# Output projection on scaled fp16 parts, attention outputs scaled one part later, and fp16 dummies at the beginning

## The chip, the cores and the metric

One Trainium2 chip, one NeuronCore. The metric is the device time of one execution in microseconds, the median of several runs. The kernel before took 1050.61 us, median of 3 runs between 1050.59 and 1055.38.

## The reference

One decoder layer for 512 prompt tokens, 16 learned meta tokens before them and 32 sample tokens (8 sequences of 4), 2048 features, everything in fp32:

```python
hn   = rmsnorm(h, pre_norm_w)                        # over 2048 features
proj = einsum('btd,de->bte', hn, w_in)               # 2048 -> 8192, in 8 parts of 1024
q, fz, i, za, bg, cg, xt, zb = split(proj)
# A: 8 heads, key and value width 128: a gated linear recurrence
f = lb + (1 - lb) * sigmoid(fz);  k = (1 - lb) * sigmoid(-fz);  v = i
S_t = diag(f_t) S_{t-1} + k_t v_t^T;   o_t = S_t^T q_t
o = rmsnorm(o, hgrn_norm_w) * silu(za)               # per head
# B: a causal convolution of width 3 over the tokens
yb = bg * conv3(cg * xt) * silu(zb)
mix = einsum('bte,ed->btd', concat([o, yb]), w_out)  # 2048 -> 2048
y = h + rmsnorm(mix, post_norm_w)
```

Returned are y for prompt and sample (without the meta tokens), and the new states of the recurrence and of the convolution.

## The kernel before

**The beginning.** Weights and tokens are loaded; the tokens are normalized and transposed on TensorE (`turn_x`, three transposes for each group of 128 features) and split into two fp16 parts, high and low. Meanwhile TensorE runs dummy matmuls (`keep_busy`) into a scratch tile `warm`: four on the second weight block as soon as that has arrived, and six on the identity after the matmul that adds up the weights' sums of squares (`scale_of_weights`). They are fp32, 128 columns wide. The first feature pair is computed on the first half of the tokens (280 columns) while the transposes still come, and then on the second half.

**The input projection** goes through 32 pairs of features (`pair`), 256 features each. Four 512 KB blocks of weights (11, 12, 21, 22) per pair are loaded by SP two pairs ahead (`load_pair`). Their squares are summed on ScalarE (`squares`), a matmul with ones (`scale_of_weights`, name pss) adds them up over the partitions, and VectorE makes a power of two of it, the scale (sc). Each block, or sum of blocks, is then scaled and split into two fp16 tiles: the high part on ScalarE, the low part on VectorE (`split_w`, L288 and L289). A product is three fp16 matmuls for each of 8 groups of 128 features (high by high, high by low, low by high: L351, L352, L353, 272 columns of tokens). Three pairs in four use seven products instead of eight (names ma, mc, md are their accumulators, e1 to e3 and sums in `put` their copies, L370). The preparation of the next pair is cut into steps (`prep_steps`), one of them at the start of each product, some in its middle.

**The eight heads** (recurrence, norm, gate: `attend` and `gate`) run as a side program, of which `tick` executes one part every 11 feature groups, between the matmuls of the projection. In `attend` the outputs po get their per-head norm factor from GpSimd's chain of 12 small operations (zur, L861 to L864); then two parts follow (i = 0 and 1), in the first of which ScalarE scales the four blocks of outputs (sq, L879). Each part also updates the state of the samples (dss, an fp32r matmul of 512 columns, L882). The last head's and the convolutions' results go into mixf, fp32, 16 groups of 128 features by 544 tokens.

**The output projection** has 8 slices of 256 features (dp), each going through four chunks c of four feature groups. For each chunk there are two `feat` (weights stationary, 288 columns: samples and half the prompt; the result yT is transposed back later) and two `toks` (tokens stationary, 256 columns of weights). Both are three matmuls for each feature group (L1058 to L1060 in `feat`, L1066 to L1068 in `toks`), with operands of type fp32r: mh and ml are mixf's high and low part (`split`, A.copy and a subtraction), wh and wl the weights' (`prep_to`, L184 and L185, four groups of 128 input features at a time, two tiles ahead). ScalarE takes the results out (`take_feat`, and in `take` a sum of squares for the post norm), VectorE multiplies them by the post norm's weights; `turn_y` transposes yT back (yps), and the residual is added and stored at the end.

Order: the text of the program gives each engine's order, that is, what `step`, `tick` and `due` emit first comes first; but what the built program holds differs from it in places. In the kernel before, ScalarE's sums of squares of a pair's weights stand up to a whole pair ahead of the step that emits them, in between the copies of accumulators.

Of the kernel before, what the change touches and what calls it, by code (L numbers as in the profile page):

```python
# [64 lines left out]
def hymba_kernel(  # L65
# [76 lines left out]
    wts = {}  # L142
# [13 lines left out]
    def load_pair(p):  # L156
        if p < NP:
            for key in ("11", "21", "22", "12"):
                load_w(p, key)
        elif p < NP + 4:  # L160
            load_to(2 * (p - NP) + 2)

    nld = npr = 0

    def load_to(n):
        nonlocal nld
        while nld < min(n, KT):
            for kc in range(KT // KC):
                raw = wpool.tile([P, KC, P], F32, name=f"rawo_{nld}_{kc}", tag="raw", bufs=6)
                dp, c = divmod(nld * 2 + kc, 4)  # L170
                src = w_out[0][c * SEQ:(c + 1) * SEQ, dp * W:(dp + 1) * W]
                nc.sync.dma_start(wide(raw), src.rearrange("(k p) e -> p k e", p=P))
                raws.setdefault(nld, []).append(raw)
            nld += 1

    def prep_to(n):
        nonlocal npr
        load_to(n)
        while npr < min(n, KT):
            for kc in range(KT // KC):  # L180
                raw = raws[npr][kc]
                wh = wpool.tile([P, KC, P], F32R, name=f"wh_{npr}_{kc}", tag="w", bufs=8)
                wl = wpool.tile([P, KC, P], F32R, name=f"wl_{npr}_{kc}", tag="w", bufs=8)
                A.copy(wh, raw)  # L184
                V.tensor_tensor(wl, raw, wh.bitcast(F32), op=ALU.subtract)  # L185
                wts.setdefault(npr, []).append((wh, wl))
            raws.pop(npr)
            npr += 1
# [76 lines left out]
    def scale_of_weights(p, cols=(0, 4), tag="tr"):  # L265
# [4 lines left out]
        pool = {"tr": ps_tr, "lv": ps_lv}[tag]  # L270
# [4 lines left out]
        G.tensor_scalar(sc[:, 1:2].bitcast(I32), sc[:, 0:1].bitcast(I32), -1.0, sxk[:, 1:2], op0=ALU.mult, op1=ALU.add)  # L275
        G.tensor_scalar(sc[:, 2:3], sc[:, 1:2], -1.0, None, op0=ALU.mult)
        return sc

    scs = {}

    def seven(p):
        return p >= PLAIN and p % 4 in SEVEN

    def split_w(p, key):
# [5 lines left out]
                               w[:, 0].rearrange("p k e -> p (k e)"), op0=ALU.mult, op1=ALU.subtract)  # L290

# [8 lines left out]
    def prep_steps(p):  # L300
# [29 lines left out]
        for key in ("11", "12", "21", "22"):  # L330
            yield lambda key=key: split_w(p, key)
# [44 lines left out]
    def pair(p, off, sink):  # L376
# [3 lines left out]
        nxt = list(prep_steps(p + 1)) if p + 1 < NP else [lambda: None] * 5 + [lambda: prep_to(1), lambda: prep_to(2)]  # L380
        due = iter(nxt)
# [102 lines left out]
    keep_busy(4, raws[0, "12"][:, 0, :])  # L484
    sc0 = scale_of_weights(0, (0, 2))
    keep_busy(6)
# [179 lines left out]
    def attend(h, f, kb, q, vt, g):  # L666
# [207 lines left out]
        for i in range(2):  # L874
            yield
            if i == 0:
# [29 lines left out]
        for hf in range(2):  # L906
            V.scalar_tensor_tensor(groups(mixf[:, h, 0:NS])[:, :, hf], groups(mps2[:, 0:NS])[:, :, hf], hnw,
                                   g[:, hf * (TH - 8):hf * (TH - 8) + 16].rearrange("p (g r) -> p g r", r=8),
                                   op0=ALU.mult, op1=ALU.mult)

    def conv(c, p0):
# [58 lines left out]
        for hf in range(2):  # L970
            V.tensor_tensor(mixf[:, 8 + c, 0:NS].rearrange("p (g h r) -> p g h r", h=2, r=8)[:, :, hf],
                            two(y)[:, hf, 0:16].rearrange("p (g r) -> p g r", r=8),
                            two(gz)[:, hf, 0:16].rearrange("p (g r) -> p g r", r=8), op=ALU.mult)

    for i in range(H):
        head(i, 4 * i, f0 if i == 0 else None)
        conv(i, 4 * i + 2)
# [6 lines left out]
    mh = [opa.tile([P, NOUT], F32R, name=f"mh{e}") for e in range(EARLY)]  # L984
    ml = [opa.tile([P, NOUT], F32R, name=f"ml{e}") for e in range(EARLY)]

    def split(e):
        A.copy(mh[e], mixf[:, e, :])
        V.tensor_tensor(ml[e], mixf[:, e, :], mh[e].bitcast(F32), op=ALU.subtract)

    for e in range(EARLY):
        split(e)
    xin.close()
    op = ctx.enter_context(tc.tile_pool(name="op", bufs=1, side="right"))
    mh += [op.tile([P, NOUT], F32R, name=f"mh{e}") for e in range(EARLY, KT)]
    ml += [op.tile([P, NOUT], F32R, name=f"ml{e}") for e in range(EARLY, KT)]
    for e in range(EARLY, KT):
        split(e)
# [253 lines left out]
```

## Time and profile before

| | |
|---|---|
| runs | 1050.61 us median (1050.59 to 1055.38) |
| profiled execution | 1055.29 us, span 1053.5 us, mean granted clock of TensorE 0.995 |
| TensorE matmul busy | 1006.8 us, 96% |
| TensorE weight load busy | 855.2 us, 81% |
| VectorE, ScalarE, GpSimd busy | 772.3 us, 607.2 us, 98.7 us |
| output projection, L1058, L1059, L1060 | 256 matmuls each, 288 columns, fp32r, mean 297, 296, 296 ns from start to end |
| output projection, L1066, L1067, L1068 | 256 matmuls each, 256 columns, fp32r, mean 285, 280, 280 ns |
| input projection, L351, L352, L353 | 1040 matmuls each, fp16, mean 279 to 282 ns |
| sums of squares of weights, L263, ScalarE | 120, mean 1058 ns, idle before them 82.9 us |

Matmuls overlap: one of 280 to 297 ns from start to end is followed by the next after some 116 to 133 ns, so their cost is the distance from start to start. A busy share says how much of a stretch an engine was at work; what it waits for is read from the idle time ahead of an instruction and its releaser.

### The profile page before, as it was taken

What the parts mean: (1) busy time and instruction counts of PE and PEld (TensorE: products, weight loads), DVE (VectorE), ACT (ScalarE), POOL (GpSimd) and SP (SyncE); (2) the same over time, 40 slices, a digit from 0 to 9 for tenths busy, and PEclk for the clock granted to TensorE, in tenths of its full rate; (3) what the DMA queues carried; (4) which work ended last, traced back from release to release, by engine and by line L of the source; (5) the groups of instructions that cost most, each with busy time, mean ns of one, the idle gap of its engine ahead of it and who ended that gap; (6) DMA issues with size and microseconds to landing.
All of it is one profiled execution on the core that took longest, in us unless ns stands there. A gap on an engine that the chain in (4) does not pass through costs nothing.

```text
span 1053.5 us, 20364 instructions
## 1 busy us (share of the span) xinstructions
PE 1006.8 (96%) x8180; PEld 855.2 (81%) x8180; DVE 772.3 (73%) x1588; ACT 607.2 (58%) x1152; POOL 98.7 (9%) x225
## 2 busy tenths in 40 slices
PE   4999899899999999999999999999999999999995
PEld 3668677788788877887787888788878899999995
DVE  6578995789789888988897898889789562222227
ACT  4488655575676667557756766675575352223223
POOL 1401001000200020011001000200110110000004
PEclk9999999999999999999999999999999999999998
DMA  9324231342242244224422422342343272322104
GB/s 309 89 59 122 81 81 36 111 137 79 70 136 80 84 121 126 69 84 118 130 81 74 130 82 84 120 138 65 83 120 121 84 251 92 110 81 91 51 1 170
DMA packets 156932, 109.35 MB, mean 104 GB/s; under 512 B 3729, under 2 KB 151362, under 8 KB 155766
## 3 DMA queue, kind: packets, MB, share of 16 engines
q1 hardware_dynamic: 152934, 92.90, 30.0%
q0 software_dynamic: 3680, 14.49, 4.1%
q8 instruction: 64, 1.05, 0.4%
q10 hardware_dynamic: 224, 0.66, 0.2%
q14 instruction: 30, 0.25, 0.1%
HBM read 98.79 MB, written 9.25 MB: 103 GB/s over the span
## 4 chain that ended last, share of the span: by engine, by line
PE 54%; DVE 21%; ACT 11%; DMA 7%; issue 4%; POOL 2%; DVEq 0%; ACTq 0%; POOLq 0%; SPq 0%
DMA raw<-in_w_in_dram 6%; DVE w L289 5%; PE mm L351 4%; PE mm L352 4%; PE mm L353 4%; DVE ws L289 3%; PE omm L1059 3%; PE omm L1060 3%; PE omm L1058 3%; ACT w L288 3%; ACT junk L263 3%; PE omm L1067 3%; PE omm L1068 3%; PE omm L1066 3%; PE ma L351 2%
## 5 line engine op out<-in xcount | busy, mean ns | idle before, releaser
L351 PE MATMUL mm<-x_b,w 128*128 128x272 f16 (+2 forms) x720 | 201.5, 280 | 0.0
L353 PE MATMUL mm<-x_b,w 128*128 128x272 f16 (+2 forms) x720 | 201.2, 279 | 0.0
L352 PE MATMUL mm<-x_b,w 128*128 128x272 f16 (+2 forms) x720 | 201.2, 279 | 0.0
L263 ACT ACTIVATE junk<-raw 128x1024 uint8<-128x1024 f32 x120 | 127.0, 1058 | 82.9 <-DMA raw<-in_w_in_dram 82.6
L289 DVE SCALAR_TENSOR_TENSOR w<-raw,sc,w 128x1024 f16<-128x1024 f32 x104 | 132.6, 1283 | 42.9 <-ACT w L288 42.5
L288 ACT ACTIVATE w<-raw,sc 128x1024 f16<-128x1024 f32 x104 | 116.6, 1139 | 47.3 <-DVE sc L241 47.3
L351 PEld LDWEIGHTS <-w 128*128 128x128 f16 x1200 | 118.3, 99 | 24.7 <-issue 1.3
L353 PEld LDWEIGHTS <-w 128*128 128x128 f16 x1200 | 117.4, 98 | 22.5
L352 PEld LDWEIGHTS <-w 128*128 128x128 f16 x1200 | 117.5, 98 | 21.3
L351 PE MATMUL ma<-x_t,ws 128*128 128x272 f16 (+2 forms) x320 | 90.3, 282 | 12.4 <-ACT e L370 12.2
L185 DVE TENSOR_TENSOR wl<-rawo,wh 128x1024 fp32r<-128x1024 f32 x32 | 39.1, 1223 | 81.3 <-ACT wh L184 81.3
L288 ACT ACTIVATE ws<-s,sc 128x1024 f16<-128x1024 f32 x60 | 68.8, 1146 | 48.9 <-DVE s L298 48.9
L353 PE MATMUL ma<-x_t,ws 128*128 128x272 f16 (+2 forms) x320 | 90.3, 282 | 0.0
L352 PE MATMUL ma<-x_t,ws 128*128 128x272 f16 (+2 forms) x320 | 90.3, 282 | 0.0
L352 PEld LDWEIGHTS <-ws 128*128 128x128 f16 x640 | 62.7, 98 | 26.0 <-issue 14.9
L289 DVE SCALAR_TENSOR_TENSOR ws<-s,sc,ws 128x1024 f16<-128x1024 f32 x60 | 76.7, 1278 | 7.2 <-ACT ws L288 7.1
L184 ACT CAST wh<-rawo 128x1024 fp32r<-128x1024 f32 x32 | 33.5, 1047 | 76.6 <-PE omm L1067 71.7
L1058 PE MATMUL omm<-mh,wh 128*128 128x288 f32 x256 | 76.0, 297 | 0.0
L1059 PE MATMUL omm<-ml,wh 128*128 128x288 f32 x256 | 75.8, 296 | 0.0
L351 PEld LDWEIGHTS <-ws 128*128 128x128 f16 x640 | 64.4, 101 | 14.0 <-issue 2.2
L1060 PE MATMUL omm<-mh,wl 128*128 128x288 f32 x256 | 75.7, 296 | 0.0
L1066 PE MATMUL omm<-wh,mh 128*128 128x256 f32 x256 | 73.0, 285 | 0.0
(319 smaller groups left out, 2595.2 us busy)
## 6 DMA issues: line engine op xcount, KB each, us to landing
raw<-in_w_in_dram SPq DMA_DIRECT2D x128, 512.0 KB, 4.5
rawo<-in_w_out_dram SPq DMA_DIRECT2D x32, 512.0 KB, 3.4
xp<-in_x_prompt_dram SPq DMA_DIRECT2D x4, 1024.0 KB, 10.5
s<-in_state_hgrn_dram POOLq DMA_DIRECT2D x8, 512.0 KB, 4.3
out_dram<-s POOLq DMA_DIRECT2D x8, 512.0 KB, 4.4
xres<-in_x_prompt_dram POOLq DMA_DIRECT2D x4, 1024.0 KB, 9.0
out_dram<-big SPq DMA_DIRECT2D x7, 256.0 KB, 2.6
wpo<-in_post_norm_w_dram POOLq DMA_DIRECT2D x4, 256.0 KB, 4.5
```

The source lines that it names most:

```text
L184: A.copy(wh, raw)
L185: V.tensor_tensor(wl, raw, wh.bitcast(F32), op=ALU.subtract)
L263: A.activation(junk, raws[p, key].rearrange("p k e -> p (k e)"), AF.Square, accum_out=t[:, c:c + 1])
L288: A.activation(w[:, 0], raw, AF.Copy, scale=s)
L289: V.scalar_tensor_tensor(w[:, 1].rearrange("p k e -> p (k e)"), raw.rearrange("p k e -> p (k e)"), s, w[:, 0].rearrange("p k e -> p (k e)" ...
L351: T.matmul(o, w[:, 0, k, :], xh, start=first, stop=False, skip_group_check=onto)
L352: T.matmul(o, w[:, 0, k, :], xl, start=False, stop=False, skip_group_check=onto)
L353: T.matmul(o, w[:, 1, k, :], xh, start=False, stop=last, skip_group_check=onto)
L1058: T.matmul(o, wh[:, s_], mh[e][:, 0:SA], start=(e == 0), stop=False)
L1059: T.matmul(o, wh[:, s_], ml[e][:, 0:SA], start=False, stop=False)
L1060: T.matmul(o, wl[:, s_], mh[e][:, 0:SA], start=False, stop=(e == KT - 1))
L1066: T.matmul(o, mh[e][:, s_], wh, start=(e == 0), stop=False)
```

## The change

- **Output projection.** Its weights go the way of the input projection's: four blocks per slice, sums of squares, a power of two as scale, and a split into two fp16 tiles, one slice ahead, a step or more at each chunk. mixf is scaled too, by a power of two from the sum of squares of 14 of its 16 feature groups (`square_of_mixed`, `scale_of_mixed`). Groups 7 and 15 (`LATE`: the last head and the last convolution) stay fp32r, mixf's part as well as the weights' (`split_late`); they use the same scales. `take` and `take_feat` multiply the scales back.
- **Pairs.** `pair` takes its steps straight from the generator `prep_steps`, of the first output slice's weights too; before, the last pair had a list of its own with `prep_to` at its end. The steps of the other pairs are the same, but some of ScalarE's sums of squares stand at other places of the built order.
- **Attention.** The four blocks of outputs are scaled in the second of the two last parts (i == 1).
- **Beginning.** The dummies are one fp32 matmul on the first weight block as soon as it is there and 6 fp16 matmuls of 512 columns, one on the second block and 5, and 7 after the scale.

```diff
+    idle = xo["t2"][:, 0, 0:2].rearrange("p k t -> p (k t)")
+    G.memset(idle, 1.0)
-    def keep_busy(n, at=ident):
+    def keep_busy(n, at=None):
+        if at is not None:
+            T.matmul(warm[:, 0:P], at, ident, start=True, stop=True)
         for _ in range(n):
-            T.matmul(warm[:, 0:P], at, ident, start=True, stop=True)
+            T.matmul(warm, idle[:, 0:P], idle[:, 0:SEQ], start=True, stop=True)
...
-    keep_busy(4, raws[0, "12"][:, 0, :])
+    keep_busy(6, raws[0, "11"][:, 0, :])
+    keep_busy(5, raws[0, "12"][:, 0, :])
     sc0 = scale_of_weights(0, (0, 2))
-    keep_busy(6)
+    keep_busy(7)
...
         load_pair(p + 2)
-        nxt = list(prep_steps(p + 1)) if p + 1 < NP else [lambda: None] * 5 + [lambda: prep_to(1), lambda: prep_to(2)]
-        due = iter(nxt)
+        due = prep_steps(p + 1)
...
+    def square_of_mixed(e):
+        if e not in LATE:
+            A.activation(junk[:, 0:NOUT], mixf[:, e, :], AF.Square, accum_out=ssm[:, e:e + 1])
...
+    def split_late(p, key):
+        if key[1] == "1":
+            return
...
+        w = wrs[p][:, i]
+        A.activation(w[:, 0], raw, AF.Copy, scale=s)
+        V.scalar_tensor_tensor(w[:, 1], raw, s, w[:, 0].bitcast(F32), op0=ALU.mult, op1=ALU.subtract)
...
         for i in range(2):
             yield
-            if i == 0:
+            if i == 1:
                 for j in range(4):
...
+    def split(pool, e):
+        t = pool.tile([P, 2, NOUT], F32R if e in LATE else F16, name=f"m{e}")
+        mh[e], ml[e] = t[:, 0], t[:, 1]
+        A.activation(mh[e], mixf[:, e, :], AF.Copy, scale=smk[:, 0:1])
...
-            wh, wl = wts[n0 + 2 * dp + c // 2][c % 2]
-            yield 4 * c + k, wide(wh)[:, k, :], wide(wl)[:, k, :]
+            w = ws[NP + dp, KEYS[c]]
+            if 4 * c + k in LATE:
+                yield 4 * c + k, wrs[NP + dp][:, c // 2, 0], wrs[NP + dp][:, c // 2, 1]
+            else:
+                yield 4 * c + k, wide(w[:, 0])[:, k, :], wide(w[:, 1])[:, k, :]
...
-        A.copy(yT, o)
+        A.activation(yT, o, AF.Copy, scale=scs[NP + dp][0][:, 1:2])
...
+            load_pair(NP + dp + 2)
+            due = prep_steps(NP + dp + 1)
             for c in range(4):
-                if c % 2 == 0:
-                    prep_to(n0 + 2 * dp + c // 2 + 2)
+                for _ in range((1, 1, 3, 2)[c]):
+                    next(due)()
```

TensorE at the start, in the kernel before: warm is the scratch tile of the dummies, pss the sum for the scale, xt the first transposed tokens.

```order
L61 MATMUL pt_pre<-par,ones 128x1
L61 MATMUL warm<-ident,raw_0_127 128x128 x4
L61 MATMUL pss_0_201<-sq_183,ones_r 128x2
L61 MATMUL warm<-ident 128x128 x6
L61 MATMUL xt_0_229<-turned,xs 128x48
```

The same place in the changed kernel; x_t_84 is the tile of ones, raw_0_124 and raw_0_127 are the first and the second weight block.

```order
L61 MATMUL pt_pre<-par,ones 128x1
L61 MATMUL warm<-ident,raw_0_124 128x128
L61 LDWEIGHTS x_t_84
L61 MATMUL warm<-x_t_84 128x512
...
L61 MATMUL warm<-ident,raw_0_127 128x128
L61 LDWEIGHTS x_t_84
L61 MATMUL warm<-x_t_84 128x512
...
L61 MATMUL pss_0_214<-sq_187,ones_r 128x2
L61 LDWEIGHTS x_t_84
L61 MATMUL warm<-x_t_84 128x512
...
L61 MATMUL xt_0_243<-turned,xs 128x48
```

The first dummies now stand behind the first weight block instead of the second, and 18 of the 20 have 512 columns of fp16.

ScalarE around pair 16 (before): e1 to e3 are copies of accumulators, junk the sums of squares of weight blocks (the second number is the pair), w11, ws1 and so on their high parts, sq<-po the scaled outputs of a head.

```order
L263 ACTIVATE junk_150,sq_18_5717<-raw21_18_5388 128x1024
L370 ACTIVATE e1_16_5397<-ma16_5394,sc_16_0_5147 128x280
L827 COPY st_5421<-dm_5458 128x128
L370 ACTIVATE e3_16_5399<-mc16_5395,sc_16_0_5147 128x280
L288 ACTIVATE w11_17_5505<-raw11_17_5057,sc_17_0_5496 128x1024
...
L854 ACTIVATE sq_5526,ssq_673<-pso_5577 32x128
L263 ACTIVATE junk_150,sq_18_5717<-raw22_18_5390 128x1024
L879 ACTIVATE sq_5526<-po_5517,zur_5581 128x128 x4
```

The same place in the changed kernel:

```order
L393 ACTIVATE e1_16_5418<-ma16_5415,sc_16_0_5167 128x280
...
L247 ACTIVATE junk_151,sq_17_5421<-raw22_17_5081 128x1024
L247 ACTIVATE junk_151,sq_17_5421<-raw12_17_5083 128x1024
L393 ACTIVATE e3_16_5420<-mc16_5416,sc_16_0_5167 128x280
L247 ACTIVATE junk_151,sq_18_5738<-raw11_18_5407 128x1024
L247 ACTIVATE junk_151,sq_18_5738<-raw21_18_5409 128x1024
L295 ACTIVATE w11_17_5526<-raw11_17_5077,sc_17_0_5517 128x1024
...
L877 ACTIVATE sq_5547,ssq_687<-pso_5598 32x128
L295 ACTIVATE ws3_17_5646<-raw21_17_5079,sc_17_0_5517 128x1024
L247 ACTIVATE junk_151,sq_18_5738<-raw22_18_5411 128x1024
L902 ACTIVATE sq_5547<-po_5538,zur_5602 128x128 x4
```

The squares of pair 17 have moved between e1 and e3 and those of pair 18 behind e3, and a weight split (ws3) now stands between the head's last sum of squares and the scaling of its outputs.

TensorE in the output projection at feature group 7 of the first slice, before: omm are the accumulators, mh6 and ml6 mixf's parts of group 6, wh and wl the weights'.

```order
L1058 MATMUL omm_10397<-mh6_10325,wh_0_1_10201 128x288
L1059 MATMUL omm_10397<-ml6_10332,wh_0_1_10201 128x288
L1060 MATMUL omm_10397<-mh6_10325,wl_0_1_10202 128x288
L1058 MATMUL omm_10397<-mh7_10352,wh_0_1_10201 128x288
L1059 MATMUL omm_10397<-ml7_10361,wh_0_1_10201 128x288
L1060 MATMUL omm_10397<-mh7_10352,wl_0_1_10202 128x288
L1058 MATMUL omm_10398<-mh4_10323,wh_0_1_10201 128x288
```

The same place in the changed kernel; wr0 is the fp32r tile of the weights of groups 7 and 15.

```order
L1086 LDWEIGHTS w12_32_10214
L1086 MATMUL omm_10432<-m6_10388,w12_32_10214 128x288
L1087 LDWEIGHTS w12_32_10214
L1087 MATMUL omm_10432<-m6_10388,w12_32_10214 128x288
L1088 LDWEIGHTS w12_32_10214
L1088 MATMUL omm_10432<-m6_10388,w12_32_10214 128x288
L1086 MATMUL omm_10432<-m7_10396,wr0_10217 128x288
L1087 MATMUL omm_10432<-m7_10396,wr0_10217 128x288
L1088 MATMUL omm_10432<-m7_10396,wr0_10217 128x288
L1086 LDWEIGHTS w12_32_10214
L1086 MATMUL omm_10433<-m4_10382,w12_32_10214 128x288
```

Group 6 has become fp16 with weight loads of its own; group 7 keeps its three fp32r matmuls, between fp16 ones.

## Rows read from the trace of the kernel before

**Rows 1.** Stretches: start:end, us, busy by engine (instructions), granted clock, DMA share, GB/s
```profile
200.00:300.00 100.00, 98.64 (x832) 81.68 (x830) 86.00 (x176) 64.81 (x117) 7.71 (x23) 1.00 0.34 96
900.00:950.00 50.00, 50.00 (x403) 49.96 (x402) 14.27 (x19) 14.31 (x32) 0.55 (x1) 1.00 0.27 90
```

**Rows 2.** Timeline of TensorE, output projection: start, length, instruction [idle before, releaser]
```profile
854.83 0.30 PE L1058 MATMUL omm<-mh,wh 128*128 128x288 f32 x1
...
857.89 0.29 PE L1060 MATMUL omm<-mh,wl 128*128 128x288 f32 x1
858.02 0.28 PE L1066 MATMUL omm<-wh,mh 128*128 128x256 f32 x1
...
860.72 0.27 PE L1068 MATMUL omm<-wh,ml 128*128 128x256 f32 x1
```

**Rows 3.** Timeline of TensorE, input projection
```profile
187.85 0.28 PE L351 MATMUL mc<-x_t,ws 128*128 128x272 f16 x1
...
190.52 0.28 PE L353 MATMUL mc<-x_t,ws 128*128 128x272 f16 x1
```

**Rows 4.** Timeline of TensorE, one fp32r matmul between fp16 ones
```profile
829.66 0.28 PE L353 MATMUL mm<-x_b,w 128*128 128x272 f16 x1
829.68 0.48 PE L882 MATMUL dss<-vbd,kh 96*128 96x512 f32 x1
...
830.13 0.28 PE L352 MATMUL mm<-x_b,w 128*128 128x272 f16 x1
```

**Rows 5.** Timeline of TensorE, the first 57 us
```profile
15.47 2.07 PE L61 MATMUL warm<-ident,raw 128*128 128x128 f32 x8 [10.17 <-DMA raw<-in_w_in_dram]
...
18.33 2.91 PE L61 MATMUL warm<-ident 128*128 128x128 f32 x12
...
25.47 0.90 PE L61 MATMUL mm<-x_b,w 128*128 128x280 f16 x3
...
43.16 9.40 PE L61 MATMUL mm<-x_b,w 128*128 128x280 f16 x63
...
52.66 0.26 PE L61 MATMUL xt<-turned,xs 48*128 48x48 f32 x1
...
55.52 0.52 PE L61 MATMUL mm<-x_b,w 128*128 128x280 f16 x3
...
56.44 0.52 PE L61 MATMUL mm<-x_b,w 128*128 128x280 f16 x3
```

**Rows 6.** Stretches of the beginning, columns as in rows 1
```profile
20.00:45.00 25.00, 25.00 (x97) 14.72 (x97) 15.08 (x31) 15.72 (x29) 6.42 (x5) 1.00 0.53 157
...
53.00:66.00 13.00, 13.00 (x88) 8.55 (x88) 9.93 (x26) 11.42 (x24) 0.92 (x1) 1.00 0.15 42
```

**Rows 7.** Waits: engine, line, releaser: us in total, times, longest
```profile
ACT junk L263 <- DMA raw<-in_w_in_dram: 82.6, 76, 2.8
...
ACT sq L879 <- POOL zur L864: 28.4, 8, 4.3
...
PE ma L351 <- ACT e L370: 12.2, 12, 2.7
```

**Rows 8.** Timeline of ScalarE ahead of a late accumulator copy
```profile
288.43 1.08 ACT L263 ACTIVATE junk<-raw 128x1024 uint8<-128x1024 f32 x1
289.38 0.23 ACT L263 ACTIVATION_READ_ACCUMULATOR junk<-raw 128x1 f32 x1
...
290.03 0.51 ACT L370 ACTIVATE e<-ma,sc 128x272 f32<-128x272 f32 x1
```

**Rows 9.** Timeline of TensorE behind two late accumulator copies
```profile
193.55 0.39 PE L351 MATMUL ma<-x_t,ws 128*128 128x272 f16 x1 [2.75 <-ACT e L370]
...
195.67 0.43 PE L353 MATMUL ma<-x_t,ws 128*128 128x272 f16 x1
195.89 0.43 PE L351 MATMUL ma<-x_t,ws 128*128 128x272 f16 x1
...
290.59 0.28 PE L351 MATMUL ma<-x_t,ws 128*128 128x272 f16 x1 [1.19 <-ACT e L370]
```

More of the change, by code (lines that the diff above doesn't have):

```diff
@@ L159, in load_pair @@
                 load_w(p, key)
[L160 to L171, printed above, removed]
-                nc.sync.dma_start(wide(raw), src.rearrange("(k p) e -> p k e", p=P))
[L173 to L188, printed above, removed]
+        elif p < NP + D // W:
+            for c, key in enumerate(KEYS):
+                raw = wpool.tile([P, KC, P], F32, name=f"rawo{key}_{p}", tag="raw", bufs=6)
+                src = w_out[0][c * SEQ:(c + 1) * SEQ, (p - NP) * W:(p - NP + 1) * W]
+                nc.sync.dma_start(wide(raw), src.rearrange("(k p) e -> p k e", p=P))
+                raws[p, key] = raw
     nc.scalar.dma_start(xs[0:NM], meta_tokens)
@@ L274, in scale_of_weights, with scale_of_mixed @@
         power(sc[:, 0:1], sc[:, 0:1], MAGIC)
-        G.tensor_scalar(sc[:, 1:2].bitcast(I32), sc[:, 0:1].bitcast(I32), -1.0, sxk[:, 1:2], op0=ALU.mult, op1=ALU.add)
+        G.tensor_scalar(sc[:, 1:2].bitcast(I32), sc[:, 0:1].bitcast(I32), -1.0, undo, op0=ALU.mult, op1=ALU.add)
         G.tensor_scalar(sc[:, 2:3], sc[:, 1:2], -1.0, None, op0=ALU.mult)
         return sc
+    ssm = const.tile([P, KT], F32, name="ssm")
+    smk = const.tile([P, 2], F32, name="smk")
+    V.memset(ssm, 0.0)
+    LATE = (H - 1, KT - 1)
+    def square_of_mixed(e):
+        if e not in LATE:
+            A.activation(junk[:, 0:NOUT], mixf[:, e, :], AF.Square, accum_out=ssm[:, e:e + 1])
+    def scale_of_mixed():
+        ps = ps_tr.tile([P, SEQ], F32, name="psm", tag="tr")
+        T.matmul(ps[:, 0:KT], ones_r.bitcast(F32), ssm, start=True, stop=True)
+        V.tensor_reduce(smk[:, 0:1], ps[:, 0:KT], axis=AX.X, op=ALU.add)
+        V.tensor_scalar(smk[:, 0:1], smk[:, 0:1], 1e-18, None, op0=ALU.max)
+        power(smk[:, 0:1], smk[:, 0:1], MAGIC)
+        V.tensor_scalar(smk[:, 1:2], smk[:, 0:1].bitcast(I32), -1.0, float(381 << 23), op0=ALU.mult, op1=ALU.add)
     scs = {}
     def seven(p):
-        return p >= PLAIN and p % 4 in SEVEN
+        return PLAIN <= p < NP and p % 4 in SEVEN
     def split_w(p, key):
@@ L983, in hymba_kernel @@
     opa = ctx.enter_context(tc.tile_pool(name="opa", bufs=1))
[L984 to L989, printed above, removed]
+    mh, ml = {}, {}
+    def split(pool, e):
+        t = pool.tile([P, 2, NOUT], F32R if e in LATE else F16, name=f"m{e}")
+        mh[e], ml[e] = t[:, 0], t[:, 1]
+        A.activation(mh[e], mixf[:, e, :], AF.Copy, scale=smk[:, 0:1])
+        V.scalar_tensor_tensor(ml[e], mixf[:, e, :], smk[:, 0:1], mh[e].bitcast(F32) if e in LATE else mh[e],
+                               op0=ALU.mult, op1=ALU.subtract)
     for e in range(EARLY):
-        split(e)
+        split(opa, e)
     xin.close()
     op = ctx.enter_context(tc.tile_pool(name="op", bufs=1, side="right"))
-    mh += [op.tile([P, NOUT], F32R, name=f"mh{e}") for e in range(EARLY, KT)]
-    ml += [op.tile([P, NOUT], F32R, name=f"ml{e}") for e in range(EARLY, KT)]
     for e in range(EARLY, KT):
-        split(e)
+        split(op, e)
     cso = op.tile([18, SEQ], F32, name="cso", tag="wpo", bufs=2)
@@ L1182, in hymba_kernel @@
                     if c == 3:
[L1183 to L1185 removed]
+                        take(ts[t], dp, 3 + t, True)
+                ws.pop((NP + dp, KEYS[c]))
+            wrs.pop(NP + dp)
         else:
[L1187 removed]
             later.append((most,))
@@ L1200, in hymba_kernel @@
                     toks(ts[t], dp, c, t)
-                take(ts[t], dp, 3 + t)
+                take(ts[t], dp, 3 + t, True)
                 for j in range(len(CUTS[3 + t])):
```

51 lines of the change are left out of this document (35 added, 16 removed).

## The prediction

> **What bounds the kernel now.** I read the stretches first, then the groups by shape, the timeline of TensorE at three places, and last the waits. From 200 us on TensorE is the bound. In an ordinary stretch of the input projection it is busy for 98.64 of 100 us, and in the output projection for 50.00 of 50, while VectorE and ScalarE work some 14 of 50 us there [rows 1]. So a shorter matmul in the output projection shortens the kernel by as much, and ScalarE and VectorE have 35 us in 50 to hide more preparation. The first 65 us are different: one step of the first token block takes 1.6 us there, the same step of the second block 0.9 us [rows 5].
>
> **Output projection.** The 1536 matmuls are three lines of 256 with 288 columns (8 slices, 16 feature groups, 2 halves) and three of 256 with 256 columns; two feature groups of 16 stay fp32r, so 672 of each width become fp16. fp32r takes 133.0 ns at 288 columns (854.83 to 857.89 us, 23 steps) and 117.4 ns at 256 (858.02 to 860.72, 23 steps) [rows 2]. fp16 at these widths isn't in the trace; at 272 columns it takes 116.1 ns (187.85 to 190.52, 23 steps) [rows 3]. Sixteen columns at 2.4 GHz are 6.7 ns, so I take 122.8 and 109.4 ns. The weight load of a step is a separate instruction that ran behind the matmuls in both. Saved: 672 x 10.2 = 6.9 us and 672 x 8.0 = 5.4 us, 12.3 us together.
>
> Against that stand the changes between fp16 and fp32r: 8 output slices x 2 groups x 4 runs, 64 islands of three fp32r matmuls. The nearest row is one fp32r matmul of 512 columns between fp16 ones: from 829.66 to 830.13 there are 0.47 us for it and two fp16 ones [rows 4]. Less 0.232 that is 0.238 us, where 512 columns are 0.213; 25 ns, of which fp32r's own surcharge (133.0 less 120) is half. From above I bound an island by a whole extra fp32r step, 0.13 us, 8.5 us in all; from below by nothing. I take 25 ns, 1.6 us, since that row is the same switch. Seven small matmuls for the weights' scale add under 0.14 us each, 1.0 us at most. The term is -9.7 us, between -12.3 and -3.
>
> The new preparation (four sums of squares, 1.2 us each with the read [rows 8], and two splits of 256 columns per output slice) adds about 6 us of ScalarE and some 1.5 us of VectorE to the 24 us of a slice; ScalarE goes from 7 to 13 us, and TensorE hides it. If that cover were gone it would cost those 6 us a slice. The feature copies and the squares of the outputs keep their count. The splits of the 16 feature groups keep their number and width, and at the hand-over both kernels wait for the last head's output, so I cost them at nothing; between -0.5 and +1.
>
> **The beginning.** The four fp32 dummies, which wait for the second weight block at 15.47 us, and the six after the scale become 1 fp32 and 6 fp16 dummies on the first weight block, 1 and 5 on the second, and 7. Each fp16 dummy is 512 columns, 0.427 us at 1.2 GHz. The last seven are 3.0 us, the six old ones took 2.9, so the transposes start no later; at worst 0.6 us later, if the first six run into the second block's arrival.
>
> What they change is the clock. The granted clock reads 1.00 there, but the spacing says otherwise: three 280-column matmuls take 0.90 us at 25.47 and 0.52 us at 55.52 [rows 5], so I go by spacing: the lower level, 1.2 GHz, until somewhere in the dense fp16 run from 43.16, and 2.4 GHz after it. What came before the rise was matmul behind matmul; the mixture of transposes and matmuls before 43.16 had not raised it. The dummies are such a dense run, from about 15.5 to 21.4 us. Once up, the clock stayed up through the same mixture: from 52.66 TensorE does only transposes until 55.52, and the three matmuls there still take 0.52 us.
>
> At full clock eleven steps (25.47 to 43.16, 1.61 us each) would take 0.92 us each, 7.6 us less. The dense run (63 matmuls in 9.4 us, at 0.119 some 7.5) gives 1.9 and the four transpose steps ahead about 1.2: 10.7 us is the most. But in 20 to 45 us ScalarE is busy for 15.72 us and VectorE for 15.08, and they would become the bound. In 53 to 66 us, the same work at full clock, ScalarE reached 11.42 of 13.00 us, 88%, with TensorE full [rows 6]. At that density 15.72 us need 17.9 instead of 25: 7 us saved, which I take. The range is 0 (no rise) to 10.7.
>
> The Trainium skill speaks against the clock here: TensorE: Matmul & The Clock Gate, Part 4 (PE-mode transpose), says that transposes don't count as busy for the clock gate. By that rule the four transpose steps after the dummies could let the clock fall again, and the saving would be only the dummies' own time and a step or two. The row at 55.52, fast right after transposes alone, does not show it.
>
> **Outputs one part later, and ScalarE's order.** ScalarE waits 28.4 us in eight places for GpSimd's chain before it scales the head's output, up to 4.3 us at once [rows 7]. The order now puts a weight split between the head's sums and that scaling, and VectorE also has splits to do meanwhile, so the wait shrinks by 1 to 2 us. What counts is whether TensorE waits: 12.2 us in 12 places for accumulator copies e [rows 7]. At 290.03 the copy stands behind a sum of squares begun at 288.43 [rows 8], and TensorE starts 1.19 us late [rows 9]. In the new order that sum has gone from ahead of the copy: up to 7 us over six heads. But in the pair before, the squares that were done early now stand, four in a row, between e1 and e3, ahead of the scale matmul that TensorE reaches 6 us after e1's product, and two more ahead of the next copy e2. I count 5.3 us for four squares and one copy, so TensorE waits 0 to 0.5 us for the scale and about 0.7 us for e2. Fourteen new squares of the mixed features, each narrower than a weight block's 1.2 us, lie in ScalarE's slack. Net I take -2 us, between -8 and +5.
>
> **Sum.** The profiled execution took 1055.3 us (span 1053.5), the median of the runs is 1050.6. The 2.75 us wait at 190.8 with the lower clock after it (some 14 matmuls 0.22 us apart instead of 0.116, 1.5 us) [rows 9] makes up 4.3 of these 4.7 us. It stands behind a square that waited for its DMA, and the new order has that copy ahead of the squares. From the profiled run: 1055.3 - 4.3 - 9.7 - 7 - 2 = 1032.3; from the median: 1050.6 - 18.7 = 1031.9. I forecast 1032 us.
>
> **Rivals.**
> The clock doesn't rise, or falls again in the transposes. For it: the mixture at 1.2 GHz did not raise it in 18 us, and the new block has ScalarE-bound gaps. Against it: 52.66 to 55.52. Then the 7 us are lost: 1039 us.
> The heads gain more: the wait for GpSimd [rows 7] goes wholly, and with it all e waits, 12 us instead of 2, and the start gains 9: 1020 to 1024 us.
> Switching is dear: an island costs 0.13 us, 8.5 instead of 1.6 us: 1039 us. For it: nothing in the trace has three fp32r matmuls in a row in an fp16 stream.
> Slower: TensorE has to wait at the scale matmul for four squares that each wait for their weight block, as 76 squares did for 82.6 us, 1.09 each [rows 7]. Then it costs 4.4 us a head, 31 us for seven, less the 2 I counted: about 1064 us. It decides from 2.7 us a head (19 us over seven). Against it: that pair's blocks are loaded a pair earlier, so they should be there.
> That the change does not do what it says has little room: the order has fp16 weight loads in the projection.
>
> **How the numbers follow.** Forecast 0.50, clock 0.22, heads gain more 0.14, dear switches 0.10, slower 0.03, both clock and switches 0.01. The forecast's own bounds give 1026 to 1037; the range reaches to the clock's and the switches' 1039 with 3 us for heads that give nothing, and down to 1022 for the better heads: 1022 to 1042. A difference under 0.5% (5.3 us) can't be told from no change here; below 1045.3 are all cases but the slower one and the worst ends of the others: faster 0.93, same 0.04, slower 0.03.
>
> **What would show it.** In the profile after: fp16 matmuls of 288 columns 122 to 124 ns apart and of 256 near 109, fp32r islands costing little more than their three steps, the output projection 9 to 11 us shorter and without TensorE idle; three 280-column matmuls at 0.52 us from the first step and phase one shorter by 6 to 8 us; e1 waits gone and small ones at e2 and at the scale. I'd be wrong if the first token block still runs at 1.6 us a step, if TensorE waits for squares in the heads, or if fp16 at 288 columns is no faster than 130 ns.

## The result and the profile after

The changed kernel took 1054.11 us, median of 20 runs (1050.72 to 1059.23), the kernel before 1046.76 us, median of 20 (1044.41 to 1055.84); the ratio, which is not the quotient of the two medians, is 1.0059 (95% interval 1.0041 to 1.0077). It became slower by 0.6%, where 1032 us were forecast. The profiled execution took 1053.44 us, span 1051.6.

A first look goes to the stretches, with the columns of [rows 1]: the output projection still never lets TensorE stand (50.00 of 50 us), but the heads do, and their mean granted clock is 0.98 instead of 1.00.

```profile
200.00:300.00 100.00, 95.61 (x791) 78.80 (x790) 83.69 (x171) 65.64 (x121) 8.73 (x23) 0.98 0.36 100
900.00:950.00 50.00, 50.00 (x432) 42.90 (x430) 18.58 (x34) 26.78 (x59) 1.48 (x5) 1.00 0.29 90
```

**Output projection.** TensorE's timeline, answering to [rows 2]. Eight fp16 steps of 288 columns take 0.98 us (854.47 to 855.45), 122 ns each; 14 of 256 columns take 1.52 us, 109 ns. An island of fp32r (855.48 to 855.83) costs no more than its steps: from the last fp16 matmul before it to the first behind it, 855.45 to 855.96, are 0.51 us, and one fp16 and three fp32r steps are 0.52. Over the islands in the trace the median is 0.52 us at 288 columns and 0.47 at 256, where the steps make 0.52 and 0.46.

```profile
852.84 0.27 PE L1094 MATMUL omm<-w,m 128*128 128x256 f16 x1
...
854.36 0.27 PE L1096 MATMUL omm<-w,m 128*128 128x256 f16 x1
854.47 0.29 PE L1086 MATMUL omm<-m,w 128*128 128x288 f16 x1
...
855.45 0.29 PE L1088 MATMUL omm<-m,w 128*128 128x288 f16 x1
855.48 0.39 PE L1086 MATMUL omm<-m,wr 128*128 128x288 f32 x1
855.71 0.29 PE L1087 MATMUL omm<-m,wr 128*128 128x288 f32 x1
855.83 0.29 PE L1088 MATMUL omm<-m,wr 128*128 128x288 f32 x1
855.96 0.30 PE L1086 MATMUL omm<-m,w 128*128 128x288 f16 x1
```

From its first to its last matmul the projection takes 190.7 us (847.85 to 1038.57) instead of 199.4 (841.85 to 1041.24): 8.7 us gained. Its first and last matmul, before and then after:

```profile
841.85 0.38 PE L1058 MATMUL omm<-mh,wh 128*128 128x288 f32 x1
...
1041.24 0.27 PE L1068 MATMUL omm<-wh,ml 128*128 128x256 f32 x1
```

```profile
847.85 0.29 PE L1086 MATMUL omm<-m,w 128*128 128x288 f16 x1
...
1038.57 0.28 PE L1096 MATMUL omm<-wr,m 128*128 128x256 f32 x1
```

Two waits early in it, at the transposes back, are in that figure already:

```profile
875.25 0.33 PE L1125 MATMUL yps<-ident,yT 128*128 128x128 f32 x1 [0.42 <-ACT yT L1100]
...
878.05 0.44 PE L1125 MATMUL yps<-ident,yT 128*128 128x128 f32 x2 [1.16 <-DVE big L1118]
```

**The beginning.** TensorE's timeline, answering to [rows 5]. The dummies end at 18.8 us, and the first three 280-column matmuls take 0.52 us; the four transpose steps between did not let the clock fall. The transpose that stood behind the first token block at 52.49 us stands at 42.79. First its line before, then the lines after:

```profile
52.49 0.23 PE L61 MATMUL pt_lb<-ident,lbp 8*128 8x8 f32 x1
```

```profile
17.17 1.67 PE L61 MATMUL warm<-x_t 128*128 128x512 f16 x7
18.77 0.26 PE L61 MATMUL xt<-turned,xs 48*128 48x48 f32 x1
...
21.83 0.52 PE L61 MATMUL mm<-x_b,w 128*128 128x280 f16 x3
...
42.79 0.23 PE L61 MATMUL pt_lb<-ident,lbp 8*128 8x8 f32 x1
```

**The heads.** From that transpose to the projection's first matmul are 805 us instead of 789. The waits (columns of [rows 7]) show a new kind, the squares of the mixed features for VectorE (L274), a new wait of TensorE at the scale (pss), and longer ones at the copies, 2.2 us each in 7 places instead of 1.0 in 12:

```profile
ACT junk L247 <- DMA raw<-in_w_in_dram: 32.2, 31, 2.3
...
ACT sq L902 <- POOL zur L887: 27.0, 8, 4.1
...
ACT junk L274 <- DVE big L995: 16.3, 7, 2.7
...
PE ma L374 <- ACT e L393: 15.6, 7, 2.4
...
PE pss L260 <- ACT junk L247: 6.3, 7, 0.9
```

One head on TensorE, the place of [rows 9]'s last row: 0.92 us at the scale, 2.42 us at the copy, and 0.9 us after the restart the matmuls are 0.22 us apart instead of 0.116. That lasts 3.41 us; the clock's record has seven such stretches between 110 and 780 us, six of them behind these waits.

```profile
256.21 0.38 PE L260 MATMUL pss<-sq,ones_r 128*128 128x4 f32 x2 [0.92 <-ACT junk L247]
...
280.51 0.28 PE L374 MATMUL ma<-x_t,ws 128*128 128x272 f16 x1 [2.42 <-ACT e L393]
...
281.65 0.43 PE L374 MATMUL ma<-x_t,ws 128*128 128x272 f16 x1
281.87 0.43 PE L375 MATMUL ma<-x_t,ws 128*128 128x272 f16 x1
```

On ScalarE, ahead of the wait at the scale, a square of mixed features waits 2.68 us for VectorE. Behind it stand the copy of a product, for which TensorE does not wait, and then the four sums of the next pair's weight squares, for which it does (the first at 251.46 us, the last ending at 256.2):

```profile
250.43 0.66 ACT L274 ACTIVATE junk<-big 128x544 uint8<-128x544 f32 x1 [2.68 <-DVE big L995]
250.99 0.19 ACT L274 ACTIVATION_READ_ACCUMULATOR junk<-big 128x1 f32 x1
251.09 0.48 ACT L393 ACTIVATE e<-ma,sc 128x280 f32<-128x280 f32 x1
251.46 1.04 ACT L247 ACTIVATE junk<-raw 128x1024 uint8<-128x1024 f32 x1
```

### The profile page after: what moved, and what is told of

It is laid out like the page before. It is cut to its first block, busy times and chain, and to the rows that moved or that the text cites. A ratio compares the mean times of both kernels' runs of the same rounds, so it can differ in the third digit from the quotient of the medians.

```text
span 1051.6 us, 20595 instructions
## 1 busy us (share of the span) xinstructions
PE 994.0 (95%) x8200; PEld 817.2 (78%) x8200; DVE 787.1 (75%) x1643; ACT 660.1 (63%) x1260; POOL 110.2 (10%) x242
## 4 chain that ended last, share of the span: by engine, by line
PE 60%; DVE 13%; ACT 13%; issue 6%; DMA 4%; POOL 3%; DVEq 0%; ACTq 0%; POOLq 0%
PE mm L374 5%; PE mm L376 5%; PE mm L375 5%; PE ma L374 5%; PE ma L376 5%; PE ma L375 5%; ACT junk L247 5%; PE omm L1087 3%; PE omm L1086 3%; PE omm L1088 3%; DVE w L296 2%; PE omm L1094 2%; PE omm L1096 2%; PE omm L1095 2%; DMA raw<-in_w_in_dram 2%
## 5 line engine op out<-in xcount | busy, mean ns | idle before, releaser
L247 ACT ACTIVATE junk<-raw 128x1024 uint8<-128x1024 f32 x120 | 126.3, 1053 | 33.1 <-DMA raw<-in_w_in_dram 32.2
L374 PE MATMUL ma<-x_t,ws 128*128 128x272 f16 (+2 forms) x320 | 93.4, 292 | 15.6 <-ACT e L393 15.6
L295 ACT ACTIVATE ws<-s,sc 128x1024 f16<-128x1024 f32 x60 | 68.8, 1147 | 52.6 <-DVE s L321 52.5
L376 PE MATMUL ma<-x_t,ws 128*128 128x272 f16 (+2 forms) x320 | 93.8, 293 | 0.0
L375 PE MATMUL ma<-x_t,ws 128*128 128x272 f16 (+2 forms) x320 | 93.6, 292 | 0.0
L375 PEld LDWEIGHTS <-ws 128*128 128x128 f16 x640 | 63.6, 99 | 28.9 <-issue 17.0
L374 PEld LDWEIGHTS <-ws 128*128 128x128 f16 x640 | 65.7, 103 | 14.5 <-issue 2.1
L376 PEld LDWEIGHTS <-ws 128*128 128x128 f16 x640 | 63.9, 100 | 13.8
L1087 PE MATMUL omm<-m,w 128*128 128x288 f16 x224 | 64.0, 286 | 0.2
L1088 PE MATMUL omm<-m,w 128*128 128x288 f16 x224 | 64.0, 286 | 0.0
L1086 PE MATMUL omm<-m,w 128*128 128x288 f16 x224 | 64.0, 287 | 0.0
L1094 PE MATMUL omm<-w,m 128*128 128x256 f16 x224 | 61.4, 274 | 0.0
L1095 PE MATMUL omm<-w,m 128*128 128x256 f16 x224 | 61.1, 273 | 0.0
```

The costliest lines, as they stand in the source:

```text
L247: A.activation(junk, raws[p, key].rearrange("p k e -> p (k e)"), AF.Square, accum_out=t[:, c:c + 1])
L295: A.activation(w[:, 0], raw, AF.Copy, scale=s)
L374: T.matmul(o, w[:, 0, k, :], xh, start=first, stop=False, skip_group_check=onto)
L375: T.matmul(o, w[:, 0, k, :], xl, start=False, stop=False, skip_group_check=onto)
L376: T.matmul(o, w[:, 1, k, :], xh, start=False, stop=last, skip_group_check=onto)
L1086: T.matmul(o, wh[:, s_], mh[e][:, 0:SA], start=(e == 0), stop=False)
```

## The experiments

All times are medians with the ratio to the kernel before on the same chip. The kernel before's median was 1046.9 us beside e1 to e4, 1046.1 beside e5 to e8, 1052.2 beside e9 to e11 and 1051.1 beside e12, so a ratio compares with those of its own group only. Three columns are worked out from each profiled execution: "first block", the start of the transpose behind the first token block (52.49 before, 42.79 after); "a head", a fifth of the time from the first matmul of pair 9 to that of pair 29, found by counting the input projection's matmuls; "projection", its first to its last matmul.

| kernel | median us (runs) | ratio (95%) | first block | a head | projection |
|---|---|---|---|---|---|
| before, profiled | | | 52.5 | 96.3 | 199.4 |
| changed | 1054.11 (20) | 1.0059 (1.0041 to 1.0077) | 42.8 | 99.1 | 190.7 |
| e1, changed, own scratch | 1052.15 (10) | 1.0042 (1.0009 to 1.0075) | 44.0 | 97.6 | 190.5 |
| e2, changed, outputs scaled early | 1052.05 (10) | 1.0045 (1.0008 to 1.0082) | 44.3 | 99.0 | 191.9 |
| e3, before + squares | 1064.20 (4) | 1.0134 (1.0070 to 1.0199) | 49.1 | 98.7 | 200.6 |
| e4, before + squares, own scratch | 1055.24 (10) | 1.0065 (1.0023 to 1.0106) | 48.9 | 97.3 | 200.7 |
| e5, changed, no squares | 1043.15 (10) | 0.9955 (0.9925 to 0.9985) | 44.5 | 96.3 | 192.0 |
| e6, before + new dummies | 1045.36 (10) | 0.9977 (0.9946 to 1.0009) | 43.6 | 96.3 | 199.4 |
| e7, before + outputs scaled later | 1050.55 (10) | 1.0037 (1.0000 to 1.0073) | 42.7 | 96.3 | 199.4 |
| e8, changed, squares deferred | 1046.51 (10) | 0.9976 (0.9940 to 1.0012) | 43.0 | 96.5 | 190.7 |
| e9, changed, squares in every 4th pair | 1040.06 (6) | 0.9894 (0.9865 to 0.9923) | 43.5 | 96.4 | 191.9 |
| e10, projection only | 1041.59 (6) | 0.9927 (0.9886 to 0.9967) | 43.9 | 96.3 | 190.7 |
| e11, changed, old dummies | 1052.39 (10) | 1.0026 (0.9997 to 1.0055) | 44.1 | 98.7 | 190.9 |
| e12, changed, wait filled | 1047.03 (10) | 0.9977 (0.9944 to 1.0011) | 44.8 | 97.7 | 190.8 |

**e1 and e4: squares of the mixed features with a scratch tile of their own.** The built order shows why the weights' squares had moved: those of pair 17, ahead of e1 before, stand behind the square of mixed features that writes the same tile `junk`. With a tile of its own for that square, as the order below shows, a weights' square stands ahead of the copy again.

```diff
-            A.activation(junk[:, 0:NOUT], mixf[:, e, :], AF.Square, accum_out=ssm[:, e:e + 1])
+            A.activation(junkm, mixf[:, e, :], AF.Square, accum_out=ssm[:, e:e + 1])
```

> The changed kernel, but the squares of the mixed features write a scratch tile of their own (544 bytes per partition) instead of the one that the weights' squares write. My theory: in the changed kernel a square of mixed features waits for a head's output, and the weights' squares, which write the same scratch tile, come behind it in the built order; so TensorE waits 1.1 us for the scale and 2.4 us (instead of 1.2) for an accumulator copy in each head, and after each 2.4 us wait the granted clock is at its lower level for 3.4 us. With a tile of its own the squares go back to the places that they have in the kernel before: no waits at the scale, 1.2 us at the copy, no or one stretch at the lower clock, and 1026 to 1033 us (kernel before 1046.8, less 9.7 for the beginning and 8.7 for the output projection, both read from the profile after). Rival, the later scaling of the attention outputs is what delays the copy: then nothing changes, 1051 to 1056 us and seven stretches at the lower clock.

> The kernel before with the squares of 14 groups of mixed features on ScalarE, written to a scratch tile of their own; their sums are used by nothing. My theory: ScalarE has the room for 14 squares of 0.66 us, the time stays at 1045 to 1049 us. Rival (ScalarE's added work as such delays the copies, whatever tile it writes): about the time of the same kernel with the shared tile, 1060 us or more.

ScalarE's built order ahead of pair 16's first copy, in e1; a square of pair 18's weights is ahead of it again:

```
L247 ACTIVATE junk_151,sq_18_5739<-raw21_18_5410 128x1024
L274 ACTIVATE junkm_682,ssm_152<-big_87 128x544
L393 ACTIVATE e1_16_5419<-ma16_5416,sc_16_0_5168 128x280
```

Both missed. The waits at the scale went and the lower clock behind the head's copy too, but a head is 97.6 and 97.3 us, still 1.0 to 1.3 above 96.3. In e1 TensorE waits for copies in 16 places, more than in either kernel: the weights' squares that stand early again wait for their DMA and hold the copy behind them. The rival in e4 (ScalarE's added work as such) had part of it. From waits, a timeline of ScalarE and the matmul that waits, in e1:

```profile
PE ma L374 <- ACT e L393: 25.1, 16, 3.7
```

```profile
301.43 1.06 ACT L247 ACTIVATE junk<-raw 128x1024 uint8<-128x1024 f32 x1 [1.87 <-DMA raw<-in_w_in_dram]
...
303.64 1.06 ACT L247 ACTIVATE junk<-raw 128x1024 uint8<-128x1024 f32 x1 [0.74 <-DMA raw<-in_w_in_dram]
...
305.20 0.48 ACT L393 ACTIVATE e<-ma,sc 128x274 f32<-128x274 f32 x1
```

```profile
305.73 0.28 PE L374 MATMUL ma<-x_t,ws 128*128 128x274 f16 x1 [1.65 <-ACT e L393]
```

**e2 and e7: the later scaling of the outputs, undone and alone.** One line, `if i == 1` against `if i == 0`.

> The changed kernel with the attention outputs scaled in the earlier of the two parts, as in the kernel before. My theory (shared scratch tile): the weights' squares stay where they are in the changed kernel, seven waits of about 2.4 us and seven stretches at the lower clock remain, 1051 to 1057 us. Rival (the later scaling delays the copy): the waits fall to 1.2 us, the clock stays up, 1028 to 1036 us.

> The kernel before with the attention outputs scaled one part later, and nothing else. My theory: three of a head's four blocks keep their place in ScalarE's order, the fourth stands two splits later; the waits for copies change by less than 0.3 us a head, 1045 to 1049 us. Rival (the later scaling delays the next copy by what stands between): 2 to 3 us a head, 1060 us or more.

The later scaling is not the cause: without it a head is 99.0, with it alone 96.3. e2 held in its time; its waits are 2.08 us, and five stretches at the lower clock remain, four of them behind the heads' copies. In e7 the 1.47 us between two matmuls at the head's copy become 1.64, 0.17 us a head, as expected there. ScalarE's wait for GpSimd, which the prediction had shrink by 1 to 2 us, is 29.3 us in eight places in e7 instead of 28.4. e7's median of 1050.55 misses its range: its ten runs lie half at 1044 to 1048 and half at 1053 to 1058 (on e6 and e11 below).

**e3: the squares alone in the kernel before.**

```diff
+    def square_of_mixed(e):
+        if e not in LATE:
+            A.activation(junk[:, 0:NOUT], mixf[:, e, :], AF.Square, accum_out=ssm[:, e:e + 1])
```

> The kernel before with one part of the change alone: the squares of 14 groups of mixed features on ScalarE, written to the weights' scratch tile; their sums are used by nothing. My theory: the seven long waits with the lower clock behind them appear here too, 2.8 us per head and some 20 us in all: 1063 to 1070 us against 1046.8. Rival (the later scaling): no such waits, 1046 to 1051 us.

Held in its time and in part in its mechanism: 98.7 us a head, 2.4 more than before (2.8 expected), with 0.9 us at the scale in each head and copies awaited for 2.08 us, but the lower clock behind only four of them. Some of its time is another thing: its first block ends at 49.1 us, and e4's at 48.9 (on e6 and e11 below). With e4, of these 2.4 us 1.4 go to the shared tile and 1.0 to the squares' own place.

**e5: no squares, a constant as their sum.** `V.memset(ssm, 50.0)`, and `square_of_mixed` returns at once.

> The changed kernel without the squares of the mixed features: a constant stands in for their sum, so the scale of the mixed features doesn't come from the data. ScalarE's built order is that of the kernel before again, with no added work in the heads. My theory (the squares in the heads, by their scratch tile and by their wait for VectorE, cost all that the change lost): the heads take what they take in the kernel before, the beginning and the output projection keep their gains, 1046.9 - 9.7 - 8.7 + 1 = 1029.5, between 1026 and 1034 us. Rival (the head start of 10 us or the later scaling disturbs the heads too): 1040 us or more, with waits for accumulator copies of 2 us or more in every head.

The heads are back to 96.3 us, so the squares are what they lost. But the time is 9 us above the range. Most of that is the gain of the beginning, which it counted on and which isn't there; e6, e7 and e11 show why. Without it the sum is 1046.1 - 8.7 + 1 = 1038.4, and the 4 to 5 us up to the median of 1043.15 stay open: the ten runs lie between 1039.08 and 1048.07, at mean granted clocks from 0.995 down to 0.982.

**e6 and e11: the dummies alone, and the changed kernel without them.**

> The kernel before with the new dummies alone. If the gain of the beginning carries through to the end: 1046.9 - 9.7 = 1037 us, between 1035 and 1040. Rival (what is gained in the first 60 us is given back in the heads, since other engines or loads are no earlier): 1043 to 1048 us.

> The changed kernel with the old dummies. If the clock in the usual run of the old dummies is up early anyway (the profiled execution of the kernel before, slow until 43 us, then stands for the few slow runs of it), the fastest runs are as fast as the changed kernel's, 1050 to 1055 us, and some of ten are 8 to 10 us above. Rival (the new dummies bring 9.7 us in the usual run): all runs at 1060 us and more.

e6 is a tie with the kernel before, and e11 is no slower than the changed kernel but for three runs of ten at 1057 to 1061 us. The profile of e7, which has the old dummies, says why: they end at 19.45 us instead of 21.24 [rows 5], the last of them at full clock, and the first 280-column matmuls take 0.52 us.

```profile
14.95 2.08 PE L61 MATMUL warm<-ident,raw 128*128 128x128 f32 x8 [9.66 <-DMA raw<-in_w_in_dram]
...
17.15 2.30 PE L61 MATMUL warm<-ident 128*128 128x128 f32 x12
...
22.07 0.52 PE L61 MATMUL mm<-x_b,w 128*128 128x280 f16 x3
```

So the old dummies can raise the clock as early as the new ones, and in the profiled execution of the kernel before they did not. The six profiles with old dummies show three courses: no rise until the dense run (before, first block to 52.5 us); an early rise that lasts (e7, e10, e11, 42.7 to 44.1); and an early rise that is lost again among transposes and matmuls (e3 and e4, 48.9 to 49.1), where the clock's record has the lower level from 28.5 us on for 13.65 us. In e3:

```profile
26.20 0.26 PE L61 MATMUL xt<-turned,xs 48*128 48x48 f32 x1 [0.98 <-DVE x_b L61]
...
27.58 0.52 PE L61 MATMUL mm<-x_b,w 128*128 128x280 f16 x3
28.68 0.34 PE L61 MATMUL xt<-turned,xs 48*128 48x48 f32 x1 [0.57 <-DVE x_b L61]
...
29.42 0.91 PE L61 MATMUL mm<-x_b,w 128*128 128x280 f16 x3
```

In the eight profiles with new dummies the first block ends at 42.8 to 44.8 us; only e9 has a fall in it, for 3.41 us at 24.80, behind a wait of 1.31. How often the old dummies fail differs: 7 of the kernel before's 31 runs beside e6 are above 1051 us, 13 of 19 beside e11 above 1048; e6 has none above 1047.85. That is what the new dummies buy in e6. They do not end the spread: 3 of the changed kernel's 20 runs take 1056 to 1059 us at mean granted clocks of 0.974 to 0.980 (the others 0.982 to 0.988), 4 of e2's 10 are 4 to 7 us above its other 6 at 0.978 to 0.981 instead of 0.988 to 0.990, and two of the three longer runs of e11, with the old dummies, look the same (0.979 and 0.980). Where the clock fell in those, no trace shows.

**e8, e9: the squares elsewhere.** e8 emits them behind the next pair's weight squares, with a tile of their own; e9 collects them and emits them in every fourth pair only, into the shared tile, and scales the outputs early.

```diff
+            if p % 4 == 3 and j == 2:
+                flush()
```

> The changed kernel with the squares of mixed features emitted a part later, behind the weights' squares of the next pair, and with a scratch tile of their own. If the wait for VectorE ahead of the square and the order of the weights' squares are the whole loss, 14 squares of 0.85 us are hidden: 1028 to 1036 us. Rival (ScalarE's place between two copies has no room for 0.85 us more): 0.8 us more wait per head than with the fixed scale, and 2.4 us waits that bring the lower clock: 1040 us or more.

> The changed kernel with two edits: the squares of the mixed features are emitted only in every fourth pair (where the built order puts them behind the weights' squares and far from the copies of the three pairs that wait for them), and the attention outputs are scaled in the earlier part again. My theory (place and waits of these squares are what the change lost, 2.4 to 2.8 us a head, and the projection keeps 7.4 to 8.9 us): heads at 96.3 us each, copies awaited for 1.4 us, no lower clock in the heads, 1037 to 1041 us. Rival (any 14 squares more on ScalarE delay the heads): 97 us or more a head, 1045 us or more.

e8 missed its range in the median: a head is short again (96.5 us), but some waits for copies are 1.7 us instead of 1.2, and its runs spread from 1039.89 to 1050.25 at mean granted clocks from 0.995 down to 0.983. e9 held. It is faster than both kernels, its slowest run (1043.08) below the fastest of the kernel before's beside it (1044.48); in its profile the head's copy is late by as much as in [rows 9], and the clock stays up behind it:

```profile
278.88 0.28 PE L380 MATMUL ma<-x_t,ws 128*128 128x272 f16 x1 [1.20 <-ACT e L399]
```

**e10: the projection's part alone** (old dummies, outputs scaled early, a constant as the sum).

> The output projection's part alone: the changed kernel with the old dummies, the outputs scaled in the earlier part, and a constant in place of the sum of the mixed features' squares (so their scale doesn't come from the data). My theory: 7.4 to 8.7 us less in the projection, 1.8 us more at the hand-over to it, heads as before: 1038 to 1041 us as the median, and some runs 8 to 10 us above it, where the clock rises late in the beginning, as in the kernel before. Rival (the projection's own preparation disturbs more than the hand-over): 1043 us or more in the fastest runs too.

Held within a microsecond (the median is 0.6 us above the range), two runs of six at 1049 and 1051 included: 8.7 us in the projection, and 77.8 us from pair 29 to its first matmul instead of 76.4.

**e12: the long wait filled.**

```diff
+            if j == 1 and p % 4 == 1 and p >= 9:
+                for _ in range(18):
+                    T.matmul(dd, ws[p, key][:, 0, 0, :], xop(xn)[0][:, 0, off:TH], start=True, stop=True)
```

> The changed kernel with 18 matmuls of 272 columns (some 2.1 us) whose result is overwritten, put on TensorE right where it waits 2.4 us for the accumulator copy in each head (pairs 9, 13, ... 29). My theory: the wait itself is no shorter, but the clock doesn't fall behind it; the six stretches of 3.41 us at the lower clock in the heads go, and with each 1.6 us: 9 to 10 us less than the changed kernel, 1044 to 1047 us. Rival (the lower clock comes from something else than TensorE standing still there, or the time saved is spent waiting for the same copies a little later): the time stays at 1051 to 1056 us.

Held in the mechanism; the gain, 7.1 us (1054.11 to 1047.03), is less than the 9 to 10 expected. TensorE does 18 idle matmuls and then waits 0.18 us for the same copy; no lower clock follows in any head of the profiled execution, with all the other waits still in it. Three of the ten runs take 1051 us at a mean granted clock of 0.985, the others 1044 to 1048 at 0.994 or more.

```profile
278.59 2.25 PE L444 MATMUL md<-x_t,ws 128*128 128x272 f16 x18
281.02 0.28 PE L374 MATMUL ma<-x_t,ws 128*128 128x272 f16 x1 [0.18 <-ACT e L393]
```

## Why the prediction was wrong

- **Output projection, -9.7 us: right.** Measured -8.7. The steps are 122 and 109 ns (122.8 and 109.4 taken), an island costs nothing over its steps (25 ns taken), and 1.6 us at two transposes (0.42 and 1.16) were not in the sum. The hand-over, taken at -0.5 to +1, is 1.4 us dearer in e10, 3.5 in the changed kernel (79.9 us from pair 29 on instead of 76.4).
- **The beginning, -7 us: the mechanism right, its size wrong by all of it in the median.** The dummies raise the clock, and against the profiled execution they gained 9.7 us. But that execution took 4.7 us more than the median that I had, and I put 4.3 of these down to the wait and the lower clock at 190.8 us [rows 9]. e7's profiled execution has that wait too, 3.55 us at 182.78 with 3.41 us of lower clock behind it, and took 1044.27 us, among the fastest. What was unusual was the beginning that I wanted to mend. The median of three that the sum started from, 1050.6, was itself 3.8 us above the median of 20. The rule of the Trainium skill that the prediction weighed (TensorE: Matmul & The Clock Gate, Part 4, PE-mode transpose) is not settled: the four transpose steps after the dummies (18.77 to 21.83) did not let the clock fall, but among transposes and matmuls it did fall in e3, e4 and e9. So the rival in which it falls again there does occur in some executions.
- **The heads, -2 us between -8 and +5: the step that failed.** It read: "Fourteen new squares of the mixed features, each narrower than a weight block's 1.2 us, lie in ScalarE's slack." They take 0.85 us each, but six of them wait 2.68 us for VectorE, and by their tile hold the weights' squares behind them, for which TensorE then waits at the scale; the head's copy, some 30 us later, comes later too. A head became 2.8 us longer: 0.9 us at the scale (0 to 0.5 taken), 1.2 more at the copy, and 1.4 from the lower clock (99.1 less 97.7 of e12), less 0.3 to 0.6 us of waits for another copy that five heads of the kernel before have (as at 318.24 us); that makes 2.9 to 3.2, a little more than was measured. From pair 9 to pair 29 it is 14 us. A tile of their own takes back 1.5 us a head (e1), another place nearly all (e9). The forecast had counted up to 7 us less at the copy, because the sum of squares ahead of it would go; it went, but between the scaling of the outputs and the copy ScalarE still takes 6.89 us (273.10 to 279.99) instead of 7.10 (282.93 to 290.03 [rows 8]), and the scaling itself waits for a longer chain on GpSimd (below). The prediction had named the sign: "if TensorE waits for squares in the heads". The scaling before, then the scaling and the copy after:

```profile
282.93 1.14 ACT L879 ACTIVATE sq<-po,zur 128x128 f32<-128x128 f32 x4 [4.22 <-POOL zur L864]
```

```profile
273.10 1.14 ACT L902 ACTIVATE sq<-po,zur 128x128 f32<-128x128 f32 x4 [4.09 <-POOL zur L887]
...
279.99 0.47 ACT L393 ACTIVATE e<-ma,sc 128x272 f32<-128x272 f32 x1
```

- **The rivals.** The slower one had the place (TensorE at the scale behind four squares) and not the mechanism: the squares wait for their turn, not for weights, which they wait for less than before (32.2 us instead of 82.6). It priced no drop of the clock. With what was measured the sum is 1046.8 - 8.7 (projection) + 17.9 (heads and hand-over: 805.1 us from the first block to the projection, 787.2 in e6) = 1056.0; the median is 1054.1.
- **What stays open.** How the copy comes 1.2 us later is shown in part. GpSimd's chain ahead of the head's output, which the copy stands behind, took 5.1 us instead of 4.1. In the kernel before one of its twelve operations takes 1.07 us where the others take 0.2; in the changed kernel two take 1.1, each beside a two-input VectorE operation:

```profile
268.25 1.14 POOL L885 TENSOR_TENSOR zur<-zur 128x5 f32<-128x5 f32 x1
...
270.04 1.09 POOL L884 TENSOR_TENSOR zur<-zur 128x5 f32<-128x5 f32 x1
```

```profile
268.07 1.27 DVE L296 SCALAR_TENSOR_TENSOR ws<-raw,sc,ws 128x1024 f16<-128x1024 f32 x1
...
269.86 1.22 DVE L321 TENSOR_TENSOR s<-s,raw 128x1024 f32<-128x1024 f32 x1
```

  That agrees with the Trainium skill (GPSIMD Engine Reference, 1. Specifications, "SBUF interfaces": contention with VectorE instructions of two SBUF inputs). In the changed kernel the longer chain would make up most of the 1.2 us, but it is not the only way: in e2 and e3 the chain takes 4.2 us, hardly more than before, and TensorE still waits 2.08 us for the copy, since ScalarE stands 1.02 us for a VectorE sum behind the scaling. In e2:

```profile
273.40 1.15 ACT L295 ACTIVATE ws<-s,sc 128x1024 f16<-128x1024 f32 x1 [1.02 <-DVE s L321]
```

```profile
279.79 0.28 PE L374 MATMUL ma<-x_t,ws 128*128 128x272 f16 x1 [2.08 <-ACT e L393]
```

  Both are gone when the squares have a scratch tile of their own (e1 and e4: chain 4.1 us, copy awaited for 1.4 and 1.2). So the shared tile brings them about; by which steps of VectorE's order was not tried.

## What to carry to other kernels

Before a stretch is mended, see that it is slow in the usual run: a profiled execution that lies above the median has something unusual in it, and it may be just that stretch. An instruction that fits into an engine's slack by its length can still cost what it waits for, and what stands behind it through a shared scratch tile; look at its place in the built order, and move it to where nobody waits. A wait of TensorE also has a price after it, if the clock falls.

## What the hardware showed

- Behind waits of TensorE of 2.42 us for the head's copy the granted clock fell to the lower level for 3.41 us in six of six (changed kernel) and in five of six (e11, 2.43 us), behind 2.08 us in four of six (e2 and e3), behind 1.2 us (before) and 1.7 us (e8) in none. The length of the wait alone doesn't decide: one of 2.84 us in e1, which ends at 501.75 us, had no fall behind it, and among the transposes of the beginning falls came behind waits of 0.57 to 1.31 us (e3, e4, e9). A fall cost about 1.4 us, and 2.25 us of idle matmuls in the wait kept the clock up.
- Three fp32r matmuls between fp16 ones cost nothing over their own steps (0.51 us where the steps make 0.52; at 256 columns 0.01 us in the median).
- The same ten fp32 dummies had the clock up by 18.7 us in one execution (e7: 0.213 us a pass until then, 0.112 behind it); in another (before) the lower clock lasted past 43 us.
